# Moving twelve blocks of the second layer's modulation behind the first layer's experts

## The chip, the cores and the metric

The kernel runs on one core of one Trainium2 chip. The metric is device time in microseconds (us) of one execution; three executions of the kernel before took 1457.76, 1460.0 and 1465.21 us, so the median is 1460.0. The engines are called PE (TensorE; its weight loads are PEld), DVE (VectorE), ACT (ScalarE), POOL (GpSimd) and SP (SyncE, which here only issues DMAs). Each engine runs its own list of instructions in order and waits on semaphores for the others.

## The reference, cut to what matters

Two layers work on 512 latent and 256 context tokens of width 1024, all in float32. Each layer first turns a conditioning vector into six modulation vectors, for latent tokens from `c` and for context tokens from `c_ctx`:

```
m = silu(cvec) @ w_mod[i] + b_mod[i]          # (1024) @ (1024, 6144)
sh1, sc1, gt1, sh2, sc2, gt2 = split(m, 6)
hl = rmsnorm(xl, g_mix) * (1 + sc1) + sh1     # then attention | SSD | Hyena, one output projection
xl = xl + gt1 * mix
h2 = rmsnorm(xl, g_ffn) * (1 + sc2) + sh2     # then 16 experts in 4 groups, top 2 of the best group
xl = xl + gt2 * moe(h2)
```

The modulation of layer 1 depends on nothing but the inputs, so it may be computed at any time before its use. Its first third (`sh1`, `sc1`) is needed when layer 1 begins; `sc2` and `gt2`, its columns 4096 to 6143, only in layer 1's second half.

## The kernel before, in words

**The modulation.** The 6144 columns of a layer are 48 blocks of 128. `adaln` (L242) computes one block `ch`: it loads the block's weights as two half tiles `mraw` of 256 KB by SP (L254) and multiplies each by 4 matmuls into 32-row parts of one PSUM bank (L256), the silu of both vectors being the stationary operand. Four blocks (AG = 4) share a bank. After the fourth, DVE copies the bank to `ms` (L260), and `adaln_end` (L233), called at the second block of the next group, folds the four parts with one small matmul (L238) and adds the bias into `mcol[l]` (L239). `affine` (L265) makes scales `ab` from columns of `mcol`.

**Where it runs.** Layer 0's first 16 blocks run in its first norm. The other 80 (32 of layer 0, 48 of layer 1) come from the iterator `fill` (L1601). `filler(n)` (L1610) takes the next n of them; the projections call it inside their matmul loops, a generator `fillers` does it between steps of attention, and `convolutions` (L1621) calls `filler(2)` (HF_ = 2) at each of its steps, woven into the attention steps by `weave` (L1671). `filler(96)` at L1672 would run what is left. All 96 blocks are done before the output projection; then `affine(0, 1)`, `affine(1, 0)` and `affine(1, 1)` follow (L1674 to L1676).

**The experts.** After out projection and routing, `experts` (L1478) runs 16 experts of up to two tiles of tokens. An expert's weights are 6 tiles of 512 KB (L1388). They go round a ring of 32 buffers: 5 of them (RE[0]) in the pool "w8r" (`wr8`, tag "re"), 27 in the pool "w8". POOL gathers token rows `xg` (L1393) and adds the results `y` into the DRAM tensor `xd` by an accumulating indirect DMA (L1474). A branch (L1790) on a count `nv` follows, for tiles that did not fit; in the profiled execution it is not taken, and each engine then runs a short leg that posts the counts which the body would have posted. On POOL that leg waits for its DMAs first.

**Between the layers.** Behind the branch SP loads two tiles `rw` of layer 1's k/v weights (L1805, L213); they lie on memory of the experts' weights. Then `combine` (L1505) reloads the six token tiles `xf` from `xd` (L1510), normalizes each (ACT squares L404 and root L406, DVE L407 and L1515), transposes them on PE (L416) and applies `ab` and `mcol` while copying out (`to_features`, L410). Layer 1's q/k/v projection follows.

**Memory and order.** SBUF pools are opened and closed as two stacks, left and right. During the experts the left stack ends with "gate", the right one with the pool "moe" of `xg`, `xh`, `g`, `gh2`, `y` and `gm`. At L1806 the pool "co" of `combine` opens on the left, over bytes that "moe" and "w8" held. A tile that lies on another's old bytes waits for that one's last users. The order of each engine's list is fixed when the program is built: a list scheduler takes what is ready first, by the program's order among the ready, and starts afresh behind a branch.

Of the kernel before, what the change touches and what calls it, by code (L numbers as in the profile page):

```python
# [10 lines left out]
F32 = mybir.dt.float32  # L11
# [7 lines left out]
P = 128  # L19
# [45 lines left out]
RE = (5, 8)  # L65
# [35 lines left out]
AG = 4  # L101
# [2 lines left out]
M0 = 5  # L104
WB = (2, 2), (2, 2)
FN = 4

GR = ((0, 2), (2, 2), (4, 2)), ((0, 3), (3, 1))
FK = (0, 3, 6)
# [31 lines left out]
def tile_kernel(tc, I, out, dbg=None):  # L141
    nc = tc.nc
    es = ExitStack()
    ACT, DVE, POOL, PE, SP = nc.scalar, nc.vector, nc.gpsimd, nc.tensor, nc.sync
# [14 lines left out]
    def bank(kind, dt=F32):  # L159
        if kind == "d" and "own" in rings:  # L160
            return rings["own"].tile([P, 512], dt, name="bank", tag="bankd", bufs=ND)
        cfg = rings["cfg"]
        i = [kind in r for r, _ in cfg].index(True)
        if cfg[i][1] == 0:
            turn[0] += 1
            i = (0, 0, 1, 0, 1, 0, 0, 1)[turn[0] % 8]
        if kind == "A":
            return rings["pool"].tile([P, 2, 512], dt, name="banks", tag=f"bank{i}", bufs=cfg[i][1] // 2)
        return rings["pool"].tile([P, 512], dt, name="bank", tag=f"bank{i}", bufs=cfg[i][1])
# [58 lines left out]
        ACT.activation(c32[:, :, 30 + v], vec[:, V_C + 8 * v:V_C + 8 * v + 8], AF.Silu)  # L228
    mcol = [const.tile([P, 48, 2], F32, name=f"mcol{l}") for l in range(DEPTH)]

    late, part = [], {}

    def adaln_end():  # L233

        while late:
            l, cs, n, ms = late.pop(0)
            pt = bank("d")
            PE.matmul(pt[:, 0:2 * n], ms, cst[:, C_SEL:C_SEL + 2 * n], start=True, stop=True)  # L238
            DVE.tensor_tensor(mcol[l][:, cs], pt[:, 0:2 * n].rearrange("p (j v) -> p j v", v=2),  # L239
                              lv(l, VL_BM, 48)[:, cs].unsqueeze(2).to_broadcast([P, n, 2]), OP.add)  # L240

    def adaln(l, ch, wp, mb, j, n, step, wp2=None):  # L242

        if j == AD:
            adaln_end()
        if j == 0:
            part["ps"] = bank("d")
        ps = part["ps"]
        for h in range(2):
            if h and wp2:  # L250
                raw = wp2.tile([P, 4, P], F32, name="mraw", tag="mraw", bufs=MB)
            else:
                raw = wp.tile([P, 4, P], F32, name="mraw", tag="mraw", bufs=mb)
            SP.dma_start(raw, I["wm"][l, :, ch, h])  # L254
            for k in range(4):
                PE.matmul(ps[32 * k:32 * k + 32, 0:P], c32[:, 4 * h + k, 30 - 2 * j:62 - 2 * j], raw[:, k],  # L256
                          start=(j + h == 0), stop=(j == n - 1 and h == 1))
        if j == n - 1:
            ms = wp.tile([P, P], F32, name="ms", bufs=2)
            DVE.tensor_copy(ms, ps[:, 0:P])  # L260
            late.append((l, slice(ch - j * step, ch + 1, step), n, ms))
# [3 lines left out]
    def affine(l, which, k=0, n=8):  # L265
        g = lv(l, (VL_GM if which == 0 else VL_GF) + k, n)
        s0 = (8 if which == 0 else 32) + k
        for v in range(2):
            DVE.scalar_tensor_tensor(ab[l][:, which, v, k:k + n], mcol[l][:, s0:s0 + n, v], 1.0, g, OP.add, OP.mult)
# [530 lines left out]
    def kv_weights(l, wp, places, lo_eng=None):  # L800

        return [split_in(wp, "w", 1072, I["wi"][l, :, WI_KV + 1072 * j:WI_KV + 1072 * (j + 1)], *WB[l], lo_eng,
                         None, "rw", places and places[j]) for j in range(2)]
# [742 lines left out]
    for l in range(DEPTH):  # L1546
# [51 lines left out]
        xb = xp.tile([P, 5, NT], F32, name="xb")  # L1598
        u = {}
        busy = {"po": False}  # L1600
        fill = iter([(0, c) for c in range(16, 48)] + [(1, c) for c in range(48)] if l == 0 else [])  # L1601

        def zeros(pool):

# [27 lines left out]
        if l == 0:  # L1632

            mixs = mxa.tile([P, 3 * NT], F32, name="mixs", tag="mixa").rearrange("p (b t) -> p b t", b=3)
            rp, close_rp = opened("rot")
            banks(B0[0])
            cf = ssd_coef(l, dtr, vp)

            def projections():
                yield from ssd_proj(l, wp, hh, hl, xb, filler)  # L1640
                yield from z_proj(l, wp, hh, hl, lambda: mixs, filler)

            weave((projections(), 1), (rotate(l, qr, rp), RW[0]), (zeros(rp), 3))
            close_rp()
            sp, close_sp = opened("ss")
            banks(B0[1])
            sg = scan(mixs)
            weave((hy_proj(l, wp, hh, hl, hy0, u, filler), 1), (sg, S0[0]), stop=0)
            close_wp()
            close_hp()  # L1650
            mx2, close_mx2 = opened("mx2", side="right")
            mixa = mx2.tile([P, 3, NT], F32, name="mixa")
            mixh = mx2.tile([P, 2, NT], F32, name="mixh")
            ak, close_ak = opened("attk", side="right")
            QT = ak.tile([P, 6, NT], F32R, name="QT")
            KT = ak.tile([P, 2, 2, NT], F32R, name="KT")
            rp, close_rp = opened("heads", side="right")
            banks(B0[2])
            weave((to_heads(l, qr, rp, QT, KT), 1), (sg, S0[1]), (fillers(), F0[0]), stop=0)
            close_rp()  # L1660
            am, close_am = opened("att", side="right")
            ag = attention(l, QT, KT, vt, am, mixa, busy)
            banks(B0[3])
            weave((sg, 1), (ag, S0[2]), (fillers(), F0[1]), stop=0)
            while busy["po"]:
                next(ag)
            close_sp()
            close_xp()
            hy, close_hy = opened("hy")
            banks(B0[4])  # L1670
            weave((ag, 1), (convolutions(), S0[3]))  # L1671
            filler(96)  # L1672
            adaln_end()
            affine(0, 1)  # L1674
            affine(1, 0)
            affine(1, 1)  # L1676
            rings["end"]()
            rings.clear()
            pd.__exit__(None, None, None)
            close_hy()  # L1680
            close_hy0()
            close_qp()
            close_vp()
            close_am()
            close_ak()
        else:
            zp, close_zp = opened("zz")
            z = zp.tile([P, 3, NLAT], F32, name="z")
            ak, close_ak = opened("attk")
            QT = ak.tile([P, 6, nt * P], F32R, name="QT")  # L1690
            KT = ak.tile([P, 2, 2, NT], F32R, name="KT")
            rp, close_rp = opened("rot")

            def projections():
                yield from ssd_proj(l, wp, hh, hl, xb, filler)
                yield from hy_proj(l, wp, hh, hl, hy0, u, filler)
                yield from z_proj(l, wp, hh, hl, lambda: z, filler)

            pg = projections()
            banks(BA)  # L1700
            cf = ssd_coef(l, dtr, vp)
            weave((rotate(l, qr, rp), 1), (to_heads(l, qr, rp, QT, KT), 1), (pg, RW[l]), stop=1)
            close_rp()
            close_qp()
            am, close_am = opened("att")
            mixa = mxa.tile([P, 3 * nt * P], F32, name="mixa", tag="mixa").rearrange("p (b t) -> p b t", b=3)
            ag = attention(l, QT, KT, vt, am, mixa, busy)
            weave((ag, PW), (pg, 1), stop=1)
            while busy["po"]:
                next(ag)  # L1710
            close_wp()
            close_hp()
            mx2, close_mx2 = opened("mx2", side="right")
            mixs = mx2.tile([P, 3, nt * P], F32, name="mixs")
            mixh = mx2.tile([P, 2, nt * P], F32, name="mixh")
            hy, close_hy = opened("hy", side="right")
            cg = convolutions()
            banks(B3)
            sp, close_sp = opened("ss")
            sg = scan(z)  # L1720
            weave((sg, 1), (ag, DW), (cg, CW))
            close_hy()
            close_sp()
            close_am()
            close_ak()
            close_zp()
            close_xp()
            close_hy0()
            close_vp()
# [69 lines left out]
        if l == 0:  # L1799
            mxa, close_mxa = opened("mxa", side="right")  # L1800
            hp, close_hp = opened("hT", side="right")
            hh = hp.tile([P, 8, NT], F32R, name="hh")
            hl = hp.tile([P, 8, NT], F32R, name="hl")
            wp, close_wp = opened("win", 2, side="right")
            wk = kv_weights(1, wp, None)  # L1805
        co, close_co = opened("co")  # L1806
        banks(BT)
        combine(l, order, gate[1], co, hh, hl)
        close_co()
        close_gp()  # L1810
        close_rt()
        close_wr8()
# [152 lines left out]
```

## Time and profile before

| what | value |
|---|---|
| median of three executions | 1460.0 us |
| profiled execution | 1466.34 us |
| its span | 1464.4 us |
| PE, DVE, ACT, POOL busy | 85%, 52%, 33%, 31% of the span |
| modulation matmuls (L256), all | 1536 records, 72.8 us of PE |
| loads of `mraw` | 192 of 256 KB |
| HBM over the span | 180 GB/s |

How to read it: the span is the time from the first to the last instruction of the profiled execution. Stages with different limits lie behind one another, so the shares are means. In the windows below, PEclk is the granted TensorE clock as a share of full speed, and the DMA share is that of the 16 DMA engines. A matmul of 32-bit floats appears as two records.

### The profile page before, as it was taken

The numbers are of one execution on the slowest core, as the hardware profiler recorded it, in microseconds if no ns is written. First come the engines' busy times: TensorE is split into PE (matmuls) and PEld (weight loads), VectorE is DVE, ScalarE is ACT, GpSimd is POOL, SyncE is SP. The second block draws the span as 40 slices with busy tenths as digits, with TensorE's granted clock in tenths as the row PEclk, the third lists the DMA queues.
The fourth block names the chain that finished last, engine by engine and source line by source line (L and its number), as shares of the span: only waits on it lengthen the run. The fifth ranks groups of instructions, "written<-read, shape, count | busy, mean of one in ns | idle before, by whom it ended". The sixth has DMA issues, their size and how long they took to land. (4 is left out here: it accounts for less than half of the span.)

```text
span 1464.4 us, 23682 instructions
## 1 busy us (share of the span) xinstructions
PE 1248.4 (85%) x8904; PEld 899.8 (61%) x8904; DVE 760.8 (52%) x1661; ACT 488.4 (33%) x1056; POOL 453.9 (31%) x497
## 2 busy tenths in 40 slices
PE   5999999899899899869998949988988888599780
PEld 2787787677677677634544428876776776345440
DVE  6854652644667875852332334754498475512121
ACT  4332334445233453311110144444454542111111
POOL 3220321544334524222323311321188412222221
PEclk9999999997799999979998969999999899699995
DMA  7744536343655163279999551111301173999954
GB/s 295 241 157 158 173 102 215 118 152 132 206 161 184 58 244 117 86 275 369 340 322 279 110 173 44 58 58 44 138 30 58 41 288 129 352 371 353 354 115 137
DMA packets 88809, 265.04 MB, mean 181 GB/s; under 512 B 10397, under 2 KB 13101, under 8 KB 88048
## 3 DMA queue, kind: packets, MB, share of 16 engines
q1 hardware_dynamic: 76016, 224.39, 43.5%
q0 software_dynamic: 12672, 39.07, 10.4%
q8 instruction: 72, 1.18, 0.3%
q14 instruction: 49, 0.40, 0.1%
HBM read 231.62 MB, written 31.79 MB: 180 GB/s over the span
## 5 line engine op out<-in xcount | busy, mean ns | idle before, releaser
L1417 PE MATMUL bank<-we,xh 128*32 128x128 f32 (+3 forms) x1280 | 208.7, 394 | 12.1 <-DVE y L1473 8.6
L1417 PEld LDWEIGHTS bank<-we,xh 128*32 128x32 f32 (+3 forms) x1280 | 99.5, 139 | 106.1 <-issue 76.9
L219 PE MATMUL bank<-hh,hw 128*128 128x512 f32 (+1 forms) x440 | 159.5, 362 | 0.1
L220 PE MATMUL bank<-hl,hw 128*128 128x512 f32 (+1 forms) x440 | 157.1, 357 | 0.0
L221 PE MATMUL bank<-hh,lw 128*128 128x512 f32 (+1 forms) x440 | 156.7, 356 | 0.4 <-DVE lw L207 0.4
L1474 POOL DMA_INDIRECT xd<-y,txi x35 | 56.6, 1618 | 177.7 <-DMA xd<-y,txi 90.2
L1417 PE MATMUL bank<-we,gh 128*32 128x256 f32 (+3 forms) x392 | 101.0, 522 | 2.8 <-ACT gh L1450 1.4
L219 PEld LDWEIGHTS bank<-hh,hw 128*128 128x128 f32 x440 | 85.4, 194 | 12.1 <-issue 1.0
L221 PEld LDWEIGHTS bank<-hh,lw 128*128 128x128 f32 x440 | 84.6, 192 | 12.8 <-DVE lw L207 0.9
L220 PEld LDWEIGHTS bank<-hl,hw 128*128 128x128 f32 x440 | 85.0, 193 | 11.4 <-issue 0.8
L930 POOL TENSOR_SCALAR pt<-pt,su 128x768 f32<-128x768 f32 (+1 forms) x60 | 55.0, 924 | 118.6 <-DVE su L929 97.6
L256 PE MATMUL bank<-mraw,c 128*32 128x128 f32 x1536 | 72.8, 295 | 16.9 <-DMA mraw<-in_wm_dram 11.8
L1393 POOL DMA_INDIRECT xg<-hd,tk x40 | 40.4, 1009 | 96.6 <-PE bank L1407 32.7
L207 DVE TENSOR_TENSOR lw<-rw,hw 128x1024 fp32r<-128x1024 f32 (+1 forms) x36 | 44.7, 1243 | 49.1 <-ACT hw L206 48.9
L256 PEld LDWEIGHTS bank<-mraw,c 128*32 128x32 f32 x1536 | 41.2, 114 | 41.4 <-DMA mraw<-in_wm_dram 16.0
L945 PE MATMUL bank<-ph,vt 128*64 128x128 f32 x624 | 53.8, 292 | 15.1 <-DVE ph L942 7.0
L1417 PEld LDWEIGHTS bank<-we,gh 128*32 128x32 f32 (+3 forms) x392 | 35.7, 143 | 49.6 <-issue 41.8
L220 PE MATMUL bank<-lo,mh 128*128 128x512 f32 x160 | 63.8, 399 | 1.5 <-DVE lo L207 1.5
L219 PE MATMUL bank<-ho,mh 128*128 128x512 f32 x160 | 64.5, 405 | 0.4 <-ACT ho L206 0.4
L221 PE MATMUL bank<-ho,ml 128*128 128x512 f32 x160 | 63.2, 395 | 0.0
L206 ACT CAST hw<-rw 128x1024 fp32r<-128x1024 f32 (+1 forms) x36 | 37.8, 1049 | 76.1 <-PE bank L220 48.0
L923 DVE TENSOR_REDUCE mx<-banks 128x1 f32<-128x768 f32 (+1 forms) x60 | 50.3, 844 | 23.3 <-PE banks L920 23.1
(478 smaller groups left out, 2744.9 us busy)
## 6 DMA issues: line engine op xcount, KB each, us to landing
we<-in_we_dram SPq DMA_DIRECT2D x192, 512.0 KB, 11.3
mraw<-in_wm_dram SPq DMA_DIRECT2D x192, 256.0 KB, 3.6
rw<-in_wi_dram SPq DMA_DIRECT2D x34, 512.0 KB, 3.5
ro<-in_wo_dram SPq DMA_DIRECT2D x16, 512.0 KB, 4.9
G<-ar SPq DMA_DIRECT2D x10, 768.0 KB, 3.9
xd<-ox SPq DMA_DIRECT2D x10, 512.0 KB, 2.7
hd<-h POOLq DMA_DIRECT2D x10, 512.0 KB, 2.9
xf<-xd SPq DMA_DIRECT2D x10, 512.0 KB, 7.0
```

What stands on the lines that cost most here:

```text
L206: ACT.copy(hi, src)
L207: (lo_eng or DVE).tensor_sub(lo, src, f(hi))
L219: PE.matmul(o, lh, rh, start=start, stop=False)
L220: PE.matmul(o, lh, rl, start=False, stop=False)
L221: PE.matmul(o, ll, rh, start=False, stop=stop)
L256: PE.matmul(ps[32 * k:32 * k + 32, 0:P], c32[:, 4 * h + k, 30 - 2 * j:62 - 2 * j], raw[:, k], start=(j + h == 0), stop=(j == n - 1 and h = ...
L923: DVE.tensor_reduce(mx, ps, axis=AX.XY, op=OP.max)
L930: POOL.tensor_scalar(pt[:, 0:nkt * P], pt[:, 0:nkt * P], su, 1.0, OP.mult, OP.mult)
L945: PE.matmul(po[64 * q:64 * q + 64, 0:P], vt[:, k0 + kt + j, h // 3], ph[:, (2 * j + q) * P:(2 * j + q + 1) * P], start=(kt + j == 0), stop ...
L1393: POOL.indirect_dma_start(out=xg[0:c], out_offset=None, in_=hd, in_offset=bass.IndirectOffsetOnAxis(ap=R.token(i)[0:c], axis=0))
L1417: PE.matmul(ps[r:r + c, 0:m], lh[:, 0:c], w[:, m * j:m * j + m], start=start, stop=stop)
L1474: POOL.indirect_dma_start(out=xd.rearrange("t (n m) -> (t n) m", n=n), out_offset=bass.IndirectOffsetOnAxis(ap=R.row(i)[r], axis=0), in_=y ...
```

## The change

The iterator `fill` ends 12 blocks earlier (NL = 12), so layer 1's blocks 36 to 47 leave the loop, and `affine(1, 1)` with them. Behind the experts' branch and the two k/v weight loads, a new pool "fill" opens on the left with 5 buffers of 512 KB and two small ones, "co" on top of it. The 12 blocks run there, in the program ahead of `combine`. Each is loaded by one DMA of 512 KB in place of two of 256 KB, in turn into the pool "w8r" (the experts' 5 ring buffers) and into "fill". Their banks are of kind "b" in place of "d". `adaln_end` and `affine(1, 1)` follow at once.

```diff
+NL = 12
-    late, part = [], {}
+    late, part, kind = [], {}, ["d"]
     def adaln_end():
-            pt = bank("d")
+            pt = bank(kind[0])
-    def adaln(l, ch, wp, mb, j, n, step, wp2=None):
+    def adaln(l, ch, wp, mb, j, n, step, wp2=None, whole=None):
         if j == 0:
-            part["ps"] = bank("d")
+            part["ps"] = bank(kind[0])
         ps = part["ps"]
+        if whole:
+            raw8 = whole.tile([P, 1024], F32, name="mr8", tag="re", bufs=RE[0])
+            SP.dma_start(raw8, I["wm"][l, :, ch].rearrange("p h a b -> p (h a b)"))
         for h in range(2):
-            if h and wp2:
+            if whole:
+                raw = raw8[:, 512 * h:512 * h + 512].rearrange("p (a b) -> p a b", a=4)
+            elif h and wp2:
...
-            SP.dma_start(raw, I["wm"][l, :, ch, h])
+            if not whole:
+                SP.dma_start(raw, I["wm"][l, :, ch, h])
...
-        fill = iter([(0, c) for c in range(16, 48)] + [(1, c) for c in range(48)] if l == 0 else [])
+        fill = iter([(0, c) for c in range(16, 48)] + [(1, c) for c in range(48 - NL)] if l == 0 else [])
...
             affine(1, 0)
-            affine(1, 1)
+            if NL <= 8:
+                affine(1, 1)
...
             wk = kv_weights(1, wp, None)
+        if l == 0:
+            fl, close_fl = opened("fill")
         co, close_co = opened("co")
         banks(BT)
+        if l == 0:
+            kind[0] = "b"
+            for j, c in enumerate(range(48 - NL, 48)):
+                adaln(1, c, fl, 0, c % AG, AG, 1, None, (wr8, fl)[j % 2])
+            adaln_end()
+            if NL > 8:
+                affine(1, 1)
         combine(l, order, gate[1], co, hh, hl)
         close_co()
+        if l == 0:
+            close_fl()
```

## Rows read from the trace of the kernel before

**Rows 1.** The page: span, and each engine's busy us, share and instructions.
```profile
span 1464.4 us, 23682 instructions
...
PE 1248.4 (85%) x8904; PEld 899.8 (61%) x8904; DVE 760.8 (52%) x1661; ACT 488.4 (33%) x1056; POOL 453.9 (31%) x497
```

**Rows 2.** Groups, 447.5 to 490: busy us, mean ns; idle before, releasers.
```profile
L256 PE MATMUL bank<-mraw,c 128*32 128x128 f32 x192 | 9.3, 280 | 1.6 <-DVE mcol L239 0.9 <-DMA mraw<-in_wm_dram 0.7
...
L238 PE MATMUL bank<-cst,ms 128*128 128x8 f32 x8 | 1.1, 215 | 0.0
```

**Rows 3.** Windows: stretch, us, busy PE PEld DVE ACT POOL, clock, DMA share, GB/s.
```profile
447.50:490.00 42.50, 40.42 (x460) 31.09 (x460) 29.68 (x67) 13.93 (x35) 16.04 (x17) 1.00 0.49 153
...
490.00:530.00 40.00, 33.74 (x272) 26.12 (x272) 34.19 (x86) 26.50 (x72) 16.15 (x27) 1.00 0.37 135
...
1130.00:1160.00 30.00, 24.30 (x183) 19.36 (x181) 18.13 (x38) 16.46 (x45) 16.16 (x15) 0.88 0.15 53
```

**Rows 4.** Timeline of PE near the experts' end: start, duration, line, operation; [idle before].
```profile
798.33 1.09 PE L1407 MATMUL bank<-cst,xg 128*128 128x128 f32 x8
...
847.72 3.67 PE L1417 MATMUL bank<-we,gh 128*96 128x512 f32 x8 [0.46 <-ACT gh L1450]
868.07 4.10 PE L416 MATMUL bank<-cst,xf 128*128 128x128 f32 x16 [16.67 <-DVE xf L1515]
```

**Rows 5.** Timeline of POOL, the last scatter into xd.
```profile
853.52 1.44 POOL L1474 DMA_INDIRECT xd<-y,txi  x1 [3.94 <-DMA xd<-y,txi]
```

**Rows 6.** Timeline of SP's DMA issues behind the branch.
```profile
851.52 0.83 SPq L213 DMA_DIRECT2D rw<-in_wi_dram  x2
860.68 2.81 SPq L1510 DMA_DIRECT2D xf<-xd  x6
863.61 1.50 SPq L213 DMA_DIRECT2D rw<-in_wi_dram  x2
```

**Rows 7.** Waits of SP, 845 to 875: total us, times, longest.
```profile
SPq L213 <- PEq L1790: 36.9, 1, 36.9
SPq L1510 <- DMA xg<-hd,tk: 8.1, 1, 8.1
```

**Rows 8.** Instructions of the branch line: min/median/max ns, first and last start.
```profile
L1790 SPq EVENT_SEMAPHORE  x9: 17/17/17, 801.6 to 814.5; - x9
...
L1790 PEldq EVENT_SEMAPHORE  x1: 51/51/51, 851.4 to 851.4; - x1
...
L1790 POOLq INC_SWDGE_SEM  x1: 1352/1352/1352, 859.1 to 859.1; - x1
```

**Rows 9.** Timeline of ACT at the start of combine.
```profile
864.00 1.06 ACT L404 ACTIVATE yb<-xf 128x1024 f32<-128x1024 f32 x1 [5.76 <-DMA xf<-xd]
...
865.17 1.28 ACT L406 ACT_TABLE_LOAD   x1
...
866.66 1.04 ACT L404 ACTIVATE yb<-xf 128x1024 f32<-128x1024 f32 x1
```

**Rows 10.** Windows, columns as in rows 3: combine, expert loads, and a thin stretch.
```profile
864.00:872.00 8.00, 3.93 (x16) 2.73 (x16) 4.11 (x10) 7.91 (x16) 0.64 (x1) 0.50 0.99 391
...
660.00:690.00 30.00, 27.77 (x88) 12.83 (x87) 8.75 (x13) 3.23 (x9) 6.96 (x5) 1.00 1.03 373
...
620.00:630.00 10.00, 3.65 (x25) 3.14 (x25) 8.92 (x43) 0.89 (x3) 0.19 (x1) 0.50 0.23 74
```

**Rows 11.** The page's DMA issues: count, KB each, median us to landing.
```profile
we<-in_we_dram SPq DMA_DIRECT2D x192, 512.0 KB, 11.3
mraw<-in_wm_dram SPq DMA_DIRECT2D x192, 256.0 KB, 3.6
```

**Rows 12.** Timeline of PE in the second tile of an expert.
```profile
654.02 7.11 PE L1417 MATMUL bank<-we,xh 128*96 128x512 f32 x16 [0.32 <-DVE xh L1409]
660.97 0.38 PE L1448 MATMUL bank<-cst,g 128*128 128x128 f32 x2
```

## The prediction

> **What bounds the kernel now.** I read the page first: the profiled execution spans 1464.4 us with TensorE (PE) busy 85% of it [rows 1]. That is a mean over stages, so I read the two places that the change touches, each by itself.
>
> *Where work is taken out.* I found the last modulation matmuls of the loop by their line (L256, tile mraw) and asked for the groups of the stretch 447.5 to 490 us. The reader is to see 192 records, which is 12 blocks of 16: exactly the blocks 36 to 47 of layer 1 that move. They occupy PE for 9.3 us, and PE waited another 1.6 us just before some of them; the small closing product of each group of four (L238) is in the same answer [rows 2]. The table of windows then says what this stretch is short of: PE 40.42 of 42.5 us (95%), VectorE (DVE) 29.68 (70%). Right behind it, when the modulation has run out and attention and convolutions go on, PE is at 33.74 of 40 (84%) and DVE at 34.19 (85%); the matching stretch of layer 1, which never had a filler, shows PE at 24.3 of 30 (81%, at clock 0.88) [rows 3]. So the fillers sit in a stretch bound by PE, and without them the same weave runs at 81 to 84% of PE.
>
> *Where work is put in.* Between the first layer's experts and its combine, the PE timeline shows the last expert product at 847.72 (it ends at 851.4) and the first transpose of combine at 868.07, with 16.7 us of nothing between [rows 4]. PE is not what ends that gap. Last there is a chain: POOL issues its last scatter into xd at 853.5 [rows 5]; SP issues the six reloads xf from 860.68 [rows 6], having waited 8.1 us [rows 7]; before that POOL's leg of the untaken branch posts its counts, from 859.1 for 1.35 us, that is until 860.45 [rows 8]; ACT's first square of xf starts at 864.00, and with a table load the second at 866.66 [rows 9]. From 864 to 872 ACT is busy 7.91 of 8 us and the DMA engines 99%, at 391 GB/s and with PE's clock at 0.50 [rows 10]. So what ends the gap is the moment at which the first xf lands, and after it ACT sets the pace.
>
> **The change part by part.**
>
> *Twelve blocks leave the loop.* They take 9.3 us of PE, and three closing products 3/4 of 1.1 = 0.8 us: 10.1 us. PE's 40.42 us in the stretch become 30.3. At 84% (the stretch behind) that lasts 35.9 us, at 81% (layer 1) 37.4, in place of 42.5: a gain of 6.6 or 5.1. I take 5.8, the middle, as both rows are the same kind of work. Ends: 0 if DVE's and ACT's chains hold the stretch where it is, 11.7 if also the 1.6 us of waits go. Their 24 loads on SP, the three copies and the three additions on DVE go too; DVE is at 70% there, so that adds nothing. What is late next is DVE, at 85% in the row behind. All that follows (output projection, router, experts) starts from the end of this stretch, so the gain is kept until the combine.
>
> *Twelve loads of 512 KB enter SP's list.* In the program they stand behind the two kv-weight loads and ahead of the six xf. Before the change, SP's order after the branch is that of the program: rw x2, xf x6, rw x2 [rows 6]. SP had nothing to do from 814.5 on (its own leg of the branch) and then stood 36.9 us in front of the first rw, until PE's leg released the experts' memory at 851.4 [rows 7, 8]. With that order kept, the new loads cannot start before 851.9 either, although the DMA engines are free by then.
>
> The first new load goes into the old ring (w8r), which PE released long ago; the second goes into the new pool "fill". That pool opens on the left stack where "co" opened before, so its first buffer lies on the bytes on which the first xf lay. The rows show what those bytes and the scatters together cost: the first xf went at 860.68. So I put the second load at 860.5, and everything behind it on SP waits with it: eight to ten more new loads, then the six xf.
>
> From there it is a queue. 512 KB at 391 GB/s [rows 10] is 1.34 us; at the 373 GB/s of a stretch full of expert loads 1.41. That queued loads pay for those ahead of them is in the landing times: 11.3 us for an expert load in a full queue, 3.6 for a modulation load of half the size [rows 11]. The first xf now lands behind 9 loads (if the last two, which need a ring slot back from PE, fall behind the first xf in SP's list) or behind 11 (if not): 9 x 1.34 = 12.1 to 11 x 1.41 = 15.5. I take 10 x 1.34 = 13.4 us later. Bounds from the nearest rows: 0, if the six xf were put first, and 15.5. Nothing later takes this back: ACT paces the six tiles as before, and the qkv of layer 1 needs them.
>
> *The matmuls, copies and additions in the gap.* 10.1 us of PE, 16 records at a time, run as each load lands, every 1.34 us; the gap is then 851.4 to about 881, so they are hidden by the loads. The last closing product and two affine operations on DVE end about when xf lands: 0 to 1 us, taken as 0. Bank kind "b" in place of "d" has three banks for six tiles in 13 us: 0. The combine's buffers move up by some 21 KB onto the experts' y and gm, released by the same scatters that xf waits for anyway: 0.
>
> *The sum.* -5.8 + 13.4 = +7.6 us. On the profiled execution, 1466.34 us (its span of 1464.4 and 1.9 around it), that gives 1474; on the median of 1460.0, from which this execution stands 0.4% off, 1467.6: I say 1468.
>
> **The rivals.**
>
> *Half of the loads go early: 1462.* The list of an engine is not always the program's order: PE runs all 16 records of an expert's first product at 654.02 and the transposes (L1448) at 660.97, where the code has L1448 between the halves [rows 12]. If SP's list were sorted so too, the loads into w8r would go from 815 on, and only five or six, those into fill, would queue ahead of xf: 5.5 x 1.34 = 7.4 - 5.8 = +1.6. Against it: at the branch all of SP's following work is put in order afresh, and before the change it came out in program order. Chance 0.13.
>
> *The loads cost nothing: 1454, not slower.* If the six xf stood ahead of the new loads in SP's list, or fill's buffers were free with PE's last use at 851.4 and ten loads went by 856, the data would land in a DMA gap and the gain of 5.8 stay (at most 11.7: 1448). It decides where the first load into fill is issued: before 854 it is this case. For it: the DMA engines have room from 814 on. Against it: the first xf's wait to 860.45. Chance 0.12.
>
> *The fillers filled holes: 1472.* If the stretch without them takes about 41 us, as DVE's and ACT's chains would have it, the gain is 1 to 2 us, the queue costs 13.4, and the sum is +12. For it: PE's wait on DVE inside the stretch. Against it: PE at 95%. Chance 0.13.
>
> *The gap keeps PE's clock up: 1465.* Combine's transposes run at clock 0.50, 16 in 4.10 us or 0.256 each; at full clock 8 take 1.09, 0.136 each [rows 4]. Were PE at its upper level (2.4 instead of 1.2 GHz) when xf lands, the 24 of 48 that ACT does not pace would need 24 x 0.12 = 2.9 us less: +7.6 - 2.9 = +4.7. For it: PE now works a little every 1.34 us in the gap. Against it: from 620 to 630 it worked in pieces too, 3.65 of 10 us, and stood at 0.50 [rows 10]. Chance 0.10. The Trainium skill (TensorE: Matmul & The Clock Gate, "HAM oscillation — how this bites in real kernels") says that PE falls to its lower clock while it waits for loads and that the remedy is to keep it occupied; by that rule the moved matmuls would help in this way; this trace shows the fall (0.50 from 864 to 872), and not yet the remedy.
>
> **How the numbers follow.** The forecast has 0.52, with a range of its own of 1463 to 1474 (12.1 to 15.5 less 3 to 9). A measurement here can tell about 0.5%, or 7.3 us. The forecast lies just beyond that, so it gives 0.32 slower and 0.20 same; holes give 0.13 slower; early halves 0.12 same and 0.01 faster; the clock 0.09 same, 0.01 slower; the loads at no cost 0.06 same and 0.06 faster. Rounded with a little for a weave that is merely sorted otherwise: faster 0.09, same 0.45, slower 0.46. The range reaches from the early case and half of the free one to the holes: 1456 to 1475.
>
> **What would show it.** The stretch of the convolutions ends 5 to 7 us earlier, with PE near 84% in it. SP issues rw x2 and one new load near 852 less the gain, then nothing until POOL's leg has ended, then nine or more new loads, then xf. The first square of ACT stands 12 to 15 us further from the last expert product than the 12.6 us it does now (851.4 to 864.0). I am wrong if new loads start before PE's last expert product, if xf is issued ahead of them, or if the stretch of the convolutions is as long as before.

## The result and the profile after

The change made the kernel slower. Four executions of the changed kernel have a median of 1473.5 us, four of the kernel before 1462.5: ratio 1.0079, 95% interval 1.0049 to 1.0108. A second measurement (e5 below) gave 1.0055, 1.0033 to 1.0077. So the change costs 8 to 12 us. The ratios are those on record, worked out from all executions, and differ a little from the quotient of two medians. The profiled execution after took 1472.5 us, only 6 more than the profiled one of before; executions of one kernel scatter by several us. I therefore compare ratios for the whole, and lengths of single steps for the causes.

An execution's time is its span and a remainder outside of it. The remainder is 1.7 to 2.1 us in every execution of the kernel before, the change, e2, e5 and e7, and 3.7 to 5.8 us in every execution of the other experiments. No run shows why. Differences of 2 to 3 us in the total can therefore not be put down to a step inside the span, and the table below gives the span by itself.

The page of the changed kernel, to be set against [rows 1]: the span grew by 6.1 us while PE worked 6 us less.
```profile
span 1470.5 us, 23664 instructions
...
PE 1242.4 (84%) x8904; PEld 893.2 (61%) x8904; DVE 765.7 (52%) x1661; ACT 488.4 (33%) x1056; POOL 455.8 (31%) x497
```

The loads. SP's timeline of the changed kernel (start, duration, line, operation), to be set against [rows 6]; `mr` is the tile of the new loads:
```profile
798.88 7.74 SPq L254 DMA_DIRECT2D mr<-in_wm_dram  x5
847.20 0.82 SPq L215 DMA_DIRECT2D rw<-in_wi_dram  x2
855.95 3.09 SPq L254 DMA_DIRECT2D mr<-in_wm_dram  x6
859.27 4.85 SPq L1519 DMA_DIRECT2D xf<-xd  x6
```
Instructions of the branch's line in the same kernel (duration ns min/median/max, first and last start), to be set against [rows 8]:
```profile
L1800 SPq COMPARE_BRANCH  x1: 73/73/73, 806.7 to 806.7; - x1
...
L1800 PEldq EVENT_SEMAPHORE  x1: 51/51/51, 847.1 to 847.1; - x1
...
L1800 POOLq INC_SWDGE_SEM  x1: 1347/1347/1347, 854.4 to 854.4; - x1
```
PE's last expert product in the same kernel, which ends at 847.07:
```profile
843.40 3.67 PE L1426 MATMUL bank<-we,gh 128*96 128x512 f32 x8 [0.46 <-ACT gh L1459]
```
The reader is to see two groups of new loads. Five, those into w8r, were issued from 798.88 to 806.62, before SP's own branch instruction (806.7) and 40 to 48 us before the experts ended. Six stand behind the branch, and they start 0.2 us after POOL's leg has ended (854.4 + 1.35 = 855.75). The xf follow them.

The combine. ACT's timeline of the changed kernel, to be set against [rows 9]:
```profile
868.24 1.06 ACT L413 ACTIVATE yb<-xf 128x1024 f32<-128x1024 f32 x1 [15.03 <-DMA xf<-xd]
...
872.07 0.29 ACT L415 ACTIVATE rs<-ss,eps 128x1 f32<-128x1 f32 x1
872.38 1.28 ACT L658 ACT_TABLE_LOAD   x1
873.68 0.21 ACT L658 ACTIVATE da<-row 128x12 f32<-128x12 f32 x1
873.79 1.04 ACT L413 ACTIVATE yb<-xf 128x1024 f32<-128x1024 f32 x1
874.74 0.19 ACT L413 ACTIVATION_READ_ACCUMULATOR yb<-xf 128x1 f32 x1
874.94 1.28 ACT L415 ACT_TABLE_LOAD   x1
```
The first square comes 21.2 us after the last expert product (847.07) and not 12.6. Between the second and the third square now stands an Exp of 12 numbers, `a = exp(A_log)` of layer 1 (L658 in `ssd_coef`, L649 before). Its order in ACT's list was not written by the change; it came with the new sorting.

The passage to the output projection. PE's timeline of the kernel before, which [rows 3] only sums up:
```profile
514.94 0.28 PE L221 MATMUL bank<-yh,fl 128*128 128x256 f32 x1
...
515.63 0.66 PE L945 MATMUL bank<-ph,vt 128*64 128x128 f32 x8
...
517.75 0.66 PE L945 MATMUL bank<-ph,vt 128*64 128x128 f32 x8 [0.66 <-DVE ph L942]
...
520.58 0.66 PE L945 MATMUL bank<-ph,vt 128*64 128x128 f32 x8 [0.88 <-ACT mh L998]
521.17 1.09 PE L275 MATMUL bank<-cst,mcol 128*128 128x128 f32 x8
...
525.54 0.48 PE L219 MATMUL bank<-ho,mh 128*128 128x512 f32 x1
```
And of the changed kernel, the same operations:
```profile
507.19 0.28 PE L223 MATMUL bank<-yh,fl 128*128 128x256 f32 x1
...
507.64 0.66 PE L954 MATMUL bank<-ph,vt 128*64 128x128 f32 x8
...
509.95 0.66 PE L954 MATMUL bank<-ph,vt 128*64 128x128 f32 x8
...
512.29 0.66 PE L954 MATMUL bank<-ph,vt 128*64 128x128 f32 x8 [0.88 <-DVE su L938]
...
513.63 0.55 PE L948 MATMUL bank<-cst,pt 128*128 128x128 f32 x3 [0.42 <-POOL pt L939]
516.54 1.12 PE L954 MATMUL bank<-ph,vt 128*64 128x128 f32 x8 [2.36 <-DVE ph L951]
517.59 1.97 PE L284 MATMUL bank<-cst,mcol 128*128 128x128 f32 x8
...
524.08 0.48 PE L221 MATMUL bank<-ho,mh 128*128 128x512 f32 x1
```
The last convolution product comes 7.75 us earlier, the first product of the output projection 1.5. Behind the last convolution product stand three groups of attention's products (`ph`) before and four after. DVE's timeline of the changed kernel shows what PE waited for:
```profile
512.23 0.61 DVE L1008 TENSOR_TENSOR ml<-mixa,mh 128x384 fp32r<-128x384 f32 x1
...
515.38 0.41 DVE L1008 TENSOR_TENSOR ml<-mixh,mh 128x256 fp32r<-128x256 f32 x1
515.71 0.68 DVE L951 COPY ph<-bank 128x512 f32<-128x512 f32 x1
```
The input of the last copy `ph` of attention was there at 514.2 (513.63 + 0.55), but eight operations of the output projection (six `ml`, two `wa`) stand ahead of it in DVE's list. PE idles 2.36 us, and its clock falls. The windows of the changed kernel (columns as in [rows 3]):
```profile
460.00:500.00 40.00, 34.22 (x292) 27.33 (x290) 29.64 (x67) 16.62 (x45) 19.84 (x22) 1.00 0.10 31
500.00:515.00 15.00, 10.98 (x90) 7.91 (x88) 13.12 (x41) 11.45 (x38) 7.51 (x17) 1.00 0.43 157
515.00:520.00 5.00, 3.46 (x20) 3.16 (x21) 2.08 (x4) 0.93 (x3) 0.00 (x0) 0.51 0.65 223
520.00:525.00 5.00, 5.00 (x34) 4.86 (x34) 4.39 (x6) 4.99 (x8) 0.00 (x0) 0.81 0.69 240
```
At 0.51, the lower of the two levels (1.2 of 2.4 GHz), the same eight attention products take 1.12 us where they took 0.66, and the first broadcast 1.97 where it took 1.09.

### The profile page after: what moved, and what is told of

The parts are those of the page before. It is cut to its first block, busy times and chain, and to the rows that moved or that the text cites. A ratio compares the mean times of both kernels' runs of the same rounds, so it can differ in the third digit from the quotient of the medians.

```text
span 1470.5 us, 23664 instructions
## 1 busy us (share of the span) xinstructions
PE 1242.4 (84%) x8904; PEld 893.2 (61%) x8904; DVE 765.7 (52%) x1661; ACT 488.4 (33%) x1056; POOL 455.8 (31%) x497
## 5 line engine op out<-in xcount | busy, mean ns | idle before, releaser
L223 PEld LDWEIGHTS bank<-hh,lw 128*128 128x128 f32 x440 | 84.5, 192 | 13.1 <-issue 0.9
L939 POOL TENSOR_SCALAR pt<-pt,su 128x768 f32<-128x768 f32 (+1 forms) x60 | 56.0, 937 | 105.3 <-DVE su L938 82.2
L265 PE MATMUL bank<-mraw,c 128*32 128x128 f32 x1344 | 61.4, 287 | 16.8 <-DMA mraw<-in_wm_dram 12.6
L929 PE MATMUL banks<-KT,QT 128*128 128x384 f32 (+1 forms) x216 | 53.4, 369 | 8.1 <-ACT pt L936 7.2
L954 PEld LDWEIGHTS bank<-ph,vt 128*64 128x64 f32 x624 | 34.9, 140 | 39.8 <-issue 15.0
```

Of the source, the lines that this page charges most:

```text
L223: PE.matmul(o, ll, rh, start=False, stop=stop)
L929: PE.matmul(ps[:, j, 0:hw], QT[:, h, qs], KT[:, h // 3, x, ks], start=(x == 0), stop=(x == 1))
L939: POOL.tensor_scalar(pt[:, 0:nkt * P], pt[:, 0:nkt * P], su, 1.0, OP.mult, OP.mult)
L954: PE.matmul(po[64 * q:64 * q + 64, 0:P], vt[:, k0 + kt + j, h // 3], ph[:, (2 * j + q) * P:(2 * j + q + 1) * P], start=(kt + j == 0), stop ...
```

## The experiments

The table holds the lengths of the steps in us, read from the PE and ACT timelines of each profile. *conv*: first to last convolution product with `gh`/`fl`; *tail*: on to attention's last product; *in*: on to the first product of the output projection; *out*: on to its last; *sum* of the four. *square*: last expert product to ACT's first square; *qkv*: first transpose of combine to the first qkv product. *span*: mean span less that of the kernel before in the same group, give or take 2 to 4 us (e6 and e12, one kernel in two groups, differ by 2.8; for the four executions of the change it is not on record). The last column is the recorded ratio to the kernel before, with its interval. e1 to e4, e5 to e8 and e9 to e12 were each timed on one chip, beside the kernel before.

| kernel | conv | tail | in | out | sum | square | qkv | span | ratio |
|---|---|---|---|---|---|---|---|---|---|
| before | 103.3 | 5.6 | 5.0 | 84.5 | 198.4 | 12.6 | 15.0 | 0 | 1 |
| after | 97.1 | 9.4 | 7.5 | 80.7 | 194.7 | 21.2 | 17.9 | - | 1.0079 (1.0049-1.0108) |
| e1 removed | 98.5 | 9.3 | 7.6 | 80.7 | 196.1 | 13.1 | 15.0 | -3.1 | 1.0000 (0.9979-1.0020) |
| e2 added | 103.2 | 5.6 | 5.0 | 84.3 | 198.1 | 23.5 | 18.0 | +11.4 | 1.0086 (1.0052-1.0119) |
| e3 w8r only | 98.2 | 9.4 | 7.5 | 80.7 | 195.7 | 12.7 | 17.1 | -3.3 | 0.9992 (0.9971-1.0014) |
| e4 Exp early | 97.9 | 9.4 | 7.4 | 80.7 | 195.3 | 21.5 | 15.3 | +7.6 | 1.0072 (1.0046-1.0098) |
| e5 after again | 98.4 | 9.4 | 7.6 | 80.8 | 196.1 | 21.8 | 17.9 | +8.8 | 1.0055 (1.0033-1.0077) |
| e6 seam | 96.4 | 7.9 | 6.4 | 82.2 | 192.8 | 21.9 | 18.7 | +3.0 | 1.0034 (1.0013-1.0056) |
| e7 w8r, seam | 98.8 | 7.9 | 6.5 | 82.2 | 195.3 | 12.8 | 17.0 | +1.5 | 1.0013 (0.9991-1.0035) |
| e8 w8r late, seam | 98.1 | 7.9 | 5.0 | 83.8 | 194.8 | 12.6 | 15.4 | -3.7 | 0.9982 (0.9965-0.9999) |
| e9 e8 again | 98.1 | 7.9 | 5.0 | 83.8 | 194.7 | 12.6 | 15.6 | -3.6 | 0.9991 (0.9967-1.0015) |
| e10 seam, Exp | 96.9 | 7.9 | 6.4 | 82.2 | 193.4 | 21.2 | 15.9 | +3.2 | 1.0037 (1.0014-1.0059) |
| e11 half loads | 97.6 | 9.4 | 7.2 | 82.3 | 196.5 | 18.4 | 16.8 | +2.3 | 1.0039 (1.0016-1.0061) |
| e12 e6 again | 98.2 | 7.9 | 5.0 | 83.8 | 194.8 | 21.2 | 18.5 | +5.8 | 1.0057 (1.0037-1.0077) |

**The two halves of the change, each alone: e1 and e2.**
```diff
 e1
+    POOL.memset(mcol[1][:, 40:48], 0.0)
...
-            for j, c in enumerate(range(48 - NL, 48)):
-                adaln(1, c, fl, 0, c % AG, AG, 1, None, (wr8, fl)[j % 2])
+            for j, c in enumerate(range(48 - NL, 40)):
+                adaln(1, c, fl, 0, c % AG, AG, 1, None, wr8)
 e2
-        fill = iter([(0, c) for c in range(16, 48)] + [(1, c) for c in range(48 - NL)] if l == 0 else [])
+        fill = iter([(0, c) for c in range(16, 48)] + [(1, c) for c in range(48)] if l == 0 else [])
...
-            if NL <= 8:
-                affine(1, 1)
+            affine(1, 1)
```


> The removal alone. The twelve blocks leave the loop as in the change; of them only the four of sc2 (36 to 39) run behind the experts, out of w8r; the eight of gt2 (40 to 47) are left out and their columns are zero, so layer 1's expert sum is multiplied by zero (routing and work stay as they are). No load lies on fill's bytes any more. Theory (the gain is real but mostly lost where the output projection begins, and the cost of the change is the queue ahead of xf): last expert product ends 4 to 5 us earlier than before (847 against 851.4), first ACT square of xf 12 to 13 us behind it, first transpose near 864, total 4 to 6 us under the kernel before, about 1457 on 1462. Rival (the fillers only filled holes, 1 to 2 us of gain): 1460 to 1462. Rival (all 8 us that the convolutions' stretch loses are kept): 1454.

> The addition alone. All 96 blocks stay in the loop as before, and blocks 36 to 47 of layer 1 are loaded and computed a second time behind the experts, as the change does it, with the same values. Theory (six loads of 512 KB queue ahead of xf on SP, 6 x 1.34 = 8.0 us, and layer 1's Exp of A_log, L658, which the list puts between the squares of xf, costs two table loads, 2.6 to 2.9 us): first ACT square of xf 21 us behind the last expert product instead of 12.6, first transpose to first qkv product 17.9 us instead of 15.0, total 10 to 11 us over the kernel before, about 1473. Rival (the queue alone counts, the table loads lie beside other work): 8 us, 1470. Rival (the moved work also disturbs what stands elsewhere): over 13 us.

e1 took 1467.9 us in the median where before took 1465.8; over all executions the ratio is 1.0000, and the interval allows 3 us of gain or loss. Inside the span e1 is 3.1 us shorter in the mean, and as much more lies outside of it (5.1 us against 2.0). The convolutions' stretch is 4.8 us shorter, but *tail* and *in* take 6.3 back. *out* then returns 3.8. PE's waits there in the kernel before (525 to 612 us: total, times, longest) have two rows that e1 and the change lose or shorten:
```profile
PE bank L1040 <- DVE xT L1037: 1.5, 1, 1.5
...
PE bank L220 <- DVE lo L207: 0.6, 1, 0.6
```
and its window behind them ran at the lower clock for part of 5 us, where the changed kernel stays at 1.00 from 525 to 612:
```profile
555.00:560.00 5.00, 5.00 (x23) 4.16 (x23) 2.59 (x7) 0.00 (x0) 2.93 (x2) 0.66 0.37 145
```
At e1 the xT wait is 0.4 and the `lo` wait is gone. The table sets the three parts side by side. e11 has the short xT wait and the fall of the clock (0.91 over the second 20 us of *out*): 82.3, so the fall is 1.6. e6, e7 and e10 have the xT wait of 1.5 and no fall: 82.2, so that wait and what goes with it is 1.5. e8, e9 and e12 have both: 83.8. Before and e2 have the `lo` wait of 0.6 besides: 84.5. Together 1.6 + 1.5 + 0.7 = 3.8.

Over the six profiles with the blocks removed and DVE's order left alone (after, e1, e3, e4, e5, e11), *sum* has a mean of 195.7, against 198.3 for before and e2. The removal is worth 2.5 us up to the output projection's end. My theory of 4 to 6 was too high; the rival of 1 to 2 is nearer.

e2 took 11 to 13 us more than before (ratio 1.0086), a little above the theory's 10 to 11: +10.9 in *square* and +3.0 in *qkv*. Of the 10.9 the end of POOL's leg makes 1.3: it comes 10.4 us behind the last expert product in e2 (861.3 + 1.35 against 852.27), 9.05 in the kernel before and 8.7 in the change. The loss is in the addition.

**Which loads cost: e3 and e11.**
```diff
 e3
-                adaln(1, c, fl, 0, c % AG, AG, 1, None, (wr8, fl)[j % 2])
+                adaln(1, c, fl, 0, c % AG, AG, 1, None, wr8)
 e11
-            SP.dma_start(raw8, I["wm"][l, :, ch].rearrange("p h a b -> p (h a b)"))
+            if ch < 41:
+                SP.dma_start(raw8, I["wm"][l, :, ch].rearrange("p h a b -> p (h a b)"))
+            else:
+                SP.dma_start(raw8[:, 0:512], I["wm"][l, :, ch, 0].rearrange("p a b -> p (a b)"))
...
-                raw = raw8[:, 512 * h:512 * h + 512].rearrange("p (a b) -> p a b", a=4)
+                o = 512 * h if ch < 41 else 0
+                raw = raw8[:, o:o + 512].rearrange("p (a b) -> p a b", a=4)
...
-                adaln(1, c, fl, 0, c % AG, AG, 1, None, (wr8, fl)[j % 2])
+                adaln(1, c, fl, 0, c % AG, AG, 1, None, wr8 if j < 5 or j == 11 else fl)
```


> The change with all twelve loads into the five buffers of w8r, none into fill. Five loads are early; in SP's list the first xf then stands ahead of the sixth, and the others lie between the xf and behind them; each needs only a buffer back from PE, which runs the first five blocks as soon as the experts end. Theory (what costs is that loads stand ahead of xf behind POOL's leg): first ACT square 12 to 14 us behind the last expert product, two to three loads of 1.34 us between the xf delay the later tiles by 3 to 4 us; the Exp of L658 stands elsewhere, so first transpose to first qkv 15 to 19 us; total 5 to 8 us under the change, about 1466. Rival (twelve loads at any place around combine cost the same DMA time): no difference to the change, 1473.

> A dose of the queue. Blocks 36 to 40 are loaded early into w8r, the six loads that stand ahead of xf (41 to 45 into fill, 47 into w8r) fetch only half of their block, 256 KB, and the half is used twice; so is 46, behind xf. Columns of gt2 come out different, which changes values and no work. Six loads stand ahead of xf as in the change, with half the bytes. Theory (xf pays for the bytes ahead of it, 512 KB in 1.34 us): last expert product to first ACT square 12.6 + 4.0 = 16.6 to 17.2 us, where the change has 21 to 22. Rival (it pays for the number of loads, or for fill's buffers being released late): 21 us as in the change. No table load of the Exp stands between the squares here, so first transpose to first qkv is 15 us; the total then is 6 to 7 us under the change, ratio about 1.000 to 1.002.

With e3 the delay of the first square is gone (12.7): the same twelve loads cost nothing there when xf stands ahead of the rest. Three loads that still stand between the xf show in *qkv*, +2.1. SP's timeline of e3 shows the order:
```profile
856.51 0.33 SPq L1519 DMA_DIRECT2D xf<-xd  x1
856.94 0.38 SPq L254 DMA_DIRECT2D mr<-in_wm_dram  x1
857.42 0.84 SPq L1519 DMA_DIRECT2D xf<-xd  x2
```
The gain over the change came out larger than the 5 to 8 us I expected: 0.9992 against 1.0055 to 1.0079, or 9 to 13 us. e11 separates two parts of the price. SP's timeline of e11:
```profile
862.99 2.78 SPq L257 DMA_DIRECT2D mr<-in_wm_dram  x6
865.88 3.85 SPq L1523 DMA_DIRECT2D xf<-xd  x6
```
and ACT's first square of it:
```profile
872.10 1.06 ACT L417 ACTIVATE yb<-xf 128x1024 f32<-128x1024 f32 x1 [11.80 <-DMA xf<-xd]
```
From the first xf issued to the first square: 3.3 us before (860.68 to 864.00), 9.0 in the change (859.27 to 868.24), 6.2 in e11. So the bytes ahead cost 5.7 us for 3 MB and 2.9 for half of them, 0.95 us for 512 KB. Added to that is the issuing itself, six instructions at 0.5 us: xf is issued 3.3 us after the first of them in the change, 2.9 in e11. My theory counted bytes alone and expected 16.6 to 17.2; the rival by number alone said 21; it was 18.4, between them. The total of e11, 1.0039, lies above the 1.002 that I expected (its span is 2.3 us longer than before, and 3 us more lie outside of it), and *qkv* at 16.8 above the 15; nothing here shows why *qkv* is longer.

**The Exp on ACT: e4 and e10.**
```diff
-        a = pool.tile([P, 12], F32, name="da")
-        ACT.activation(a, row[:, rl + R_AL:rl + R_AL + 12], AF.Exp)
+        if l == 0:
+            for i in range(DEPTH):
+                al = row[:, i * RL_N + R_AL:i * RL_N + R_AL + 12]
+                ACT.activation(al, al, AF.Exp)
+        a = row[:, rl + R_AL:rl + R_AL + 12]
```


> The change with the Exp of A_log of both layers (L658) done in layer 0's coefficients, in place in row; layer 1 has none of its own. SP's list is that of the change. Theory (the Exp between the squares costs two table loads of ACT, which sets the pace of combine): 2.6 to 2.9 us under the change, first transpose to first qkv 15.0 instead of 17.9 us, about 1470.5. Rival (ACT's table loads lie beside the wait for xf or for PE): no difference, 1473.

> The change with both the order on VectorE of e6 and the early Exp of e4; the twelve loads stand as in the change. What is left of the loss is then the queue ahead of xf. Theory (losses add up): 2.6 us under e12, ratio 1.001 to 1.003, and 5 to 6 us over e9; first transpose to first qkv near 15.2. Rival (the Exp's table loads lie beside something else, as the ratio 1.0072 of e4 would have it): equal to e12.

In the step it is shown: *qkv* is 15.3 and 15.9 with the Exp done early, 17.9 to 18.7 in the five profiles with it between the squares. In the total it is not: e10 is 2.4 us under e12 (1470.7 and 1473.0), but their intervals overlap, and e4 at 1.0072 lies between the two measurements of the change. Of e4's time 4.2 us lie outside the span, where the change has 1.9; its span is 7.6 us over the kernel before, that of e5 8.8. So the step's gain may stand inside the span, but these numbers are too wide to tell.

**The order on DVE at the passage: e5, e6, e12.**
```diff
-                (ACT.copy if kt % 4 else DVE.tensor_copy)(ph, ps)
+                cp = (ACT.copy if kt % 4 else DVE.tensor_copy)(ph, ps)
+                if kt == 0:
+                    busy["ph"] = cp
...
-            DVE.tensor_mul(wa, wr, ab[l][:, 1, v].unsqueeze(2).to_broadcast([P, 8, 32]))
+            with behind(ph):
+                DVE.tensor_mul(wa, wr, ab[l][:, 1, v].unsqueeze(2).to_broadcast([P, 8, 32]))
...
-                DVE.tensor_sub(ml[:, k0:k1], m[:, :, s], f(mh[:, k0:k1]))
+                with behind(ph if late_op["n"] else None):
+                    DVE.tensor_sub(ml[:, k0:k1], m[:, :, s], f(mh[:, k0:k1]))
```
`behind(ph)` is `tc.issue_after(ph.ins)`, which orders an engine's list behind that instruction; `late_op` counts the token tiles, so the first one's `ml` is left as it was. Layer 1 passes None.

> The changed kernel itself, as the yardstick of this group: about 11 us over the kernel before (ratio 1.007 to 1.009). Theory (the removal shortens the stretch from the first to the last convolution product by 5 to 6 us, and the passage to the first output-projection product grows by 6, so that the removal is worth nothing; the queue and the table loads remain): last convolution product to first output-projection product 16.5 to 17 us, against 10.6 in the kernel before. Rival (that passage differs from run to run): other lengths here.

> The change, with one more order for VectorE: the splits ml of the second token tile and the products wa (L1008, L993 of the changed kernel) are put behind attention's last copy ph. Nothing else is changed, and the twelve loads stand as in the change. Theory (these splits, 2.4 us, stand ahead of the copy that PE's last attention products wait for; PE then idles 2.4 us and does the broadcasts at its lower clock, which costs 2 us more): the last ph copy goes 1.5 us earlier and the passage to the first output-projection product shrinks by 2 to 4 us, total 2 to 4 us under the change. Rival (attention's own chain leaves PE thin there anyway, so the clock falls all the same): 1.5 us or less. Rival (the splits were needed there: first output product waits for them): no gain.

> The kernel of e6 once more, as the yardstick for e10: ratio 1.003 to 1.005 to the kernel before, first transpose to first qkv 17.9 to 18.7 us with the Exp's two table loads in it.

DVE's timeline of e6:
```profile
515.82 0.61 DVE L1016 TENSOR_TENSOR ml<-mixh,mh 128x256 fp32r<-128x256 f32 x1
516.80 0.69 DVE L951 COPY ph<-bank 128x512 f32<-128x512 f32 x1 [0.37 <-PE bank L948]
517.41 0.41 DVE L1000 TENSOR_TENSOR wa<-wr,ab 128x256 f32<-128x256 f32 x1
```
and PE's:
```profile
517.64 1.12 PE L956 MATMUL bank<-ph,vt 128*64 128x128 f32 x8 [0.87 <-DVE ph L951]
518.69 1.97 PE L284 MATMUL bank<-cst,mcol 128*128 128x128 f32 x8
520.45 1.21 PE L284 MATMUL bank<-cst,ab 128*128 128x128 f32 x8
```
The copy now waits for PE and not PE for eight splits: 0.87 us of idle time in place of 2.36. In this profile the clock falls all the same, but comes back one broadcast earlier. In the profile of e12, which is the same kernel, it does not fall here:
```profile
518.52 0.66 PE L956 MATMUL bank<-ph,vt 128*64 128x128 f32 x8 [0.88 <-DVE ph L951]
519.10 1.09 PE L284 MATMUL bank<-cst,mcol 128*128 128x128 f32 x8
520.03 1.04 PE L284 MATMUL bank<-cst,ab 128*128 128x128 f32 x8
```
It falls some 30 us later instead, in the second 20 us of *out*. The windows of e6 and of e12 there:
```profile
544.08:564.08 20.00, 18.51 (x121) 15.71 (x119) 12.67 (x18) 6.23 (x12) 8.98 (x7) 1.00 0.32 123
...
543.48:563.48 20.00, 18.50 (x113) 15.69 (x112) 11.75 (x18) 6.22 (x12) 8.98 (x7) 0.91 0.32 123
```
e7 and e10 are like e6, e8 and e9 like e12. A fall at the passage makes *in* 1.4 to 1.5 us longer, one in *out* makes that 1.6 longer, so the two profiles of one kernel differ by that in both columns and by 0.2 in their sum. In e8, e9 and e12 a short fall had gone ahead (0.96 over the window from 15 to 10 us before the first product of the output projection, against 1.00 in e6, e7 and e10); whether that decides the place is not shown.

*tail* and *in* lose 2.5 to 4 us together in the six profiles with this order, and *out* gives 1.5 to 3.1 of it back (some 1.5 of either spread is the place of that fall), so *sum* is 194.3 in the mean, 1.4 under those without it. In the total e6 lies 2.6 us under e5 with intervals that overlap, and e12, the same kernel again, has 1.0057 where e5 has 1.0055: a gain in the total is not shown. The order explains part of the passage; the other part (*tail* 7.9 against 5.6) remains: attention has one step more left when the convolutions end, and its steps stand 2.3 us apart (507.64, 509.95 and 512.29 in the change). No run took that part apart.

**What comes out when the losses are taken away: e7, e8, e9.** e7 is e3 with the order of e6; e8 and e9 also put the last seven blocks behind combine in the program:
```diff
-            for j, c in enumerate(range(48 - NL, 48)):
+            for c in range(48 - NL, 41):
                 adaln(1, c, fl, 0, c % AG, AG, 1, None, wr8)
-            adaln_end()
-            if NL > 8:
-                affine(1, 1)
         combine(l, order, gate[1], co, hh, hl)
+        if l == 0:
+            for c in range(41, 48):
+                adaln(1, c, fl, 0, c % AG, AG, 1, None, wr8)
+            adaln_end()
+            if NL > 8:
+                affine(1, 1)
```


> All twelve loads into w8r (as in e3) and the order on VectorE of e6. Theory (two independent losses): e3 stood at 0.999 of the kernel before; the passage gives 2 to 4 us more, so 1461 to 1463 where the kernel before takes 1465, ratio 0.997. Rival (the passage gives nothing): 0.999 again.

> As e7, but only blocks 36 to 40 stand ahead of combine in the program and 41 to 47 behind it, so that all six xf go ahead of the seven late loads on SP. Theory (in e3 the loads between the xf made first transpose to first qkv 17.1 us instead of 15.0): 15 us again, 2 us under e7, ratio 0.995 to 0.996. Rival (the seven late blocks, 0.6 us of PE each, now stand among the qkv products and cost there what they saved): equal to e7.

> The kernel of e8 once more, beside the others of this group. Theory (the removal keeps some 4 us once VectorE's order is mended, and the loads cost nothing behind xf): ratio 0.997 to 0.999 to the kernel before, again. Rival (e8 fell below 1 by chance): 1.000 or above.

In e8 and e9 the six xf go first, *square* is 12.6 and *qkv* 15.4 and 15.6, as before. Their ratios, 0.9982 and 0.9991, are 2.6 and 1.3 us under the kernel before. The first interval just leaves out 1 and the second does not, so a gain in the total is likely and not shown. Inside the span both are 3.6 to 3.7 us shorter, and scatter of the executions allows 1.2 to 6.2; 1.8 us more than before lie outside of it. e8 missed the 0.995 to 0.996 that I expected, and e7 at 1.0013 the 0.997. e7 has the steps of e3 and yet a span 4.8 us longer against its own kernel before; the steps do not show where that lies.

## Why the prediction was right in its size, and where it was wrong

**The total.** Forecast +7.6 us, slower (1468 on 1460.0); measured +8 to +12, slower (1473.5 on 1462.5). The sum of measured steps is -2.5 (removal) + 8.6 to 9.2 (*square*, after and e5) + 2.9 (*qkv*) = +9.0 to +9.6. That the time came out near was luck: 3.3 us of gain too much and 2.9 of list effects left out stood against 4.2 to 4.8 of queue too much. One sum is wrong as written: 15.5 less 3 on 1460 gives 1472.5 as the upper end of the forecast's own range, not 1474.

**The removal, -5.8.** The step itself was right: *conv* is 4.5 to 6.9 us shorter in all kernels without the blocks, and PE is at 34.2 of 40 in the change (86%; I had said 84). What failed is "the gain is kept until the combine". I looked at what bounds the stretch and not at what starts when it ends: one more step of attention, a queue of splits on DVE, and PE's fallen clock. In the change *tail* and *in* grew by 6.3 us together, and *out* returned 3.8. Of 5.8 some 2.5 remain. The rival in which the fillers filled holes had nearly the right size for a wrong reason.

**The loads, +13.4.** The failing step is "with that order kept, the new loads cannot start before 851.9 either". I held, and wrote above under memory and order, that a list starts afresh behind a branch, and that SP keeps the program's order; the five w8r loads came out ahead of the branch, from 798.88. By my own criterion (new loads before PE's last expert product) the forecast's mechanism was wrong there, and the rival of the early halves, at 0.13, was right in the mechanism: six loads queue, not ten. Its time of 1462 was too low, as it took the gain of 5.8 and a price of 1.34. The rest of the step held: the first load into fill waits for the end of POOL's leg, and the xf queue behind it. The price of one was 1.34 us in my sum and 1.43 to 1.53 in *square* (8.6 and 9.2 over six), of which 0.95 is bytes and 0.5 the issue, which I had left out.

**The list effects, 0.** The sum had none on ACT; the Exp costs 2.9 us. The Trainium skill (ScalarE: Activation LUTs, "What ACT_TABLE_LOAD costs") counts a load of 1283 ns and a drain of 1380 ns for each change of set, which would make 5.3 us of these two. The trace shows the loads at 1.28 us, and no such drain: no more than 0.02 us lies ahead of each load or behind it, and *qkv* grew by 2.9.

**The clock rival, 1465.** It did not come about. While the moved blocks run, from 860 to 868, the changed kernel has a granted clock of 0.80; after 4.03 us without work before the first transpose it is at 0.50 again from 872 to 876:
```profile
860.00:868.00 8.00, 6.74 (x144) 4.88 (x136) 0.99 (x5) 0.00 (x0) 0.00 (x0) 0.80 1.03 411
...
872.00:876.00 4.00, 2.66 (x10) 1.86 (x10) 0.98 (x3) 3.92 (x7) 0.00 (x0) 0.50 1.02 408
```
The Trainium skill (TensorE: Matmul & The Clock Gate, "HAM oscillation — how this bites in real kernels") advises restructuring a loop so that PE does not wait for loads between its pieces and stays at the upper clock; here the blocks end 4 us before the first transpose, so they occupy PE in the wrong part of the gap.

**Still open.** The remainder outside the span has no cause shown, and it moves totals by 2 to 3 us; the place at which the clock falls has none either; and the attention step that is left behind the convolutions has no test.

## What to carry to other kernels

When work is taken out of a stretch that one engine fills, look at the first thing that is late when the stretch ends sooner: here one more step of attention and a queue of early splits on DVE stood there, and more than half of the gain went. Before a step's length is put down to an edit, the clock in it is to be compared: two profiles of one kernel differed by 1.5 us in *in* because the fall lay elsewhere. And where a total does not follow its steps, span and remainder are to be read apart. When loads are added near a branch or a reload, ask of each into which memory it goes and who releases that: loads into memory long free were issued early and cost these steps nothing, loads that wait for the same release as the reload stood in front of it, and each cost its issue as well as its bytes. After any such change, read ACT's list for table loads that have moved.

## What the runs showed that I had not expected

- Loads written behind the branch were issued ahead of it, 40 to 48 us before PE's last expert product ended (798.88 to 806.62 against 847.07).
- One issue of a DMA took SP 0.5 us here (six of 512 KB in 3.09, six of 256 KB in 2.78), a third of what a queued load cost the one behind it.
- PE's clock fell at the passage after 2.36 us of idle time, and in e6 after 0.87. In the kernel before PE idled 0.88 us at the same place and the eight products kept their 0.66 us, and so they did in e12, the kernel of e6, after 0.88. The idle time just ahead does not by itself tell which level follows, nor does the kernel.
